# Experts with blocks of 64 slots: raw float32 weights on two column tiles instead of split weights

## The chip, the cores and the metric

The kernel runs on one core of a Trainium2 chip. Its engines are TensorE (PE; its weight loads are a row of their own, PEld), VectorE (DVE), ScalarE (ACT), GpSimd (POOL) and SyncE (SP), which here issues the loads from HBM; 16 DMA engines carry them. The metric is the device time of one execution in microseconds (us).

## The reference, cut to what matters

Two residual layers work on 256 tokens of width 1024 in float32. The change touches only the last part, a layer of eight SwiGLU experts, two for each token:

```python
def moe_swiglu(x, router, w_gate, w_up, w_down):
    t = x.reshape(-1, d)
    top_logits, top_idx = lax.top_k((t @ router), TOP_K)          # 2 of 8
    top_w = jax.nn.softmax(top_logits, axis=-1)
    gates = jnp.sum(jax.nn.one_hot(top_idx, N_EXPERTS) * top_w[..., None], axis=1)
    for e in range(N_EXPERTS):                                    # d = 1024, 3584 inner columns
        out = out + gates[:, e:e+1] * (silu(t @ w_gate[e]) * (t @ w_up[e])) @ w_down[e]
```

The weights of the eight experts are 352 MB of float32, and each is read once.

## The kernel before

**Slots.** The experts are ranked by how many tokens chose them. A rank p has a fixed capacity, `CAPS = (128, 192, 128, 128, 64, 64, 64, 64)`, in blocks of 128 slots ("wide") and of 64 ("narrow"): ranks 0, 2 and 3 have one wide block, rank 1 a wide and a narrow one, ranks 4 to 7 a narrow one each. `gather` (L1155) picks the tokens of a block with matmuls against a 0/1 matrix S (tiles `xgw`, `xgw2` for wide blocks, parts of `fek`, `f1k`, `fak` for narrow ones).

**Order of the work.** A rank's 3584 inner columns are taken in seven column blocks f of 512. `STARTS` says at which step each rank begins; the plan made of it (L234 to L241) is a list of items ("g", p, f), ("u", p, f), ("d", p, f): gate, up and down projection of a column block. Rank 0 comes first, rank 6 joins at its sixth column block and then runs alone, then ranks 1, 4 and 5 run in turn (one column block of each is called a triple below), then 2, 3 and at last 7. Work that follows a projection (evacuations, transposes, scatters) is put some half blocks later by `later(d, ...)` and is issued at `tick()`.

**Weights.** An item reads two weight blocks of 1 MB ("chunks"), each in two halves. SP loads them into eight raw buffers (and at the start into some spare tiles) in the order of the plan; a load waits until the last reader of the buffer's old content is done. `prep` (L138) runs four halves ahead of the use: ACT copies a half, rounded, to `whi` (L146), DVE subtracts to get the rest, `wlo` (L154). PE multiplies both in its faster float32r format, so that the product has nearly full float32 precision.

**Matmuls.** The picked tokens are the stationary operand and the weights stream, 512 columns at a time. A wide block has its tokens split as well and needs three products (`wm`, L412). A narrow block holds 64 high parts and 64 low parts side by side in the 128 columns of the array, so that two products give all four (`streams`, L1198); the two halves of the result lie in different partitions and have to be added. For that each gate and up projection of a narrow block is copied by ACT (`to_rows`, L1220), transposed in four pieces on PE (`folded`, L1237) and summed by DVE's reduction (`summed`, L1242). SiLU and product (`shaped`, L1258 and L1261) and another split (`parted`, L420 and L421) follow; wide blocks are transposed in `turned` (L1267). `down` sums over the column blocks in PSUM or, for a block that "spills", in SBUF (`spilled`), and `scatter` (L1340) brings the sums back to the tokens with S transposed, after they have been split too.

Before the first layer's convolution norm there is `warm_tiles` (L777), a row of matmuls without use on array tiles of 64, 32 and 128 columns.

Of the kernel before, what the change touches and what calls it, by code (L numbers as in the profile page):

```python
# [17 lines left out]
P = 128  # L18
# [35 lines left out]

WARM_TILES = ((64, 256, 5), (32, 256, 3), (64, 512, 3), (128, 256, 2))
# [22 lines left out]
def tile_trunk(ctx: ExitStack, tc: tile.TileContext, a: dict, out: bass.AP, caps=CAPS, starts=STARTS,  # L78
# [94 lines left out]
    def use(count=1):  # L173

        n = state["use"]
        state["use"] = n + count
        if count == 1:
            end = n > 2 * len(chunks) - TAIL
            prep(n + (TAIL_HI if end else LOOK_HI), n + (TAIL_LO if end else LOOK_LO))
            return his[n], los[n]  # L180
        prep(n + count, n + count - 1)
        return [(his[m], los[m]) for m in range(n, n + count)]
# [62 lines left out]
    for p, n0 in starts:  # L245
        kept = [n for n in kept if n + NFB > n0]
        spills[p] = [bi > 0 or len(kept) == 2 for bi in range(len(_blocks(caps[p])))]
        if not spills[p][0]:
            kept.append(n0)
# [15 lines left out]
    for what, p, f in plan:  # L265
        for h in range(2):
            if what == "d":
# [503 lines left out]
    def warm_tiles():  # L771

        b = bank()
        for cols, n, times in WARM_TILES:
            for i in range(times):
                for c in range(0, P, cols):
                    te.matmul(b[c:c + cols, :n], gw[:, i % 4, c:c + cols], m0.rearrange("p g t -> p (g t)")[:, 0:n],  # L777
                              start=True, stop=True)

    def conv_norm(i):  # L780
# [3 lines left out]
        warm_tiles()  # L784
# [315 lines left out]
    def step():  # L1100
        tick()
        return use()
# [43 lines left out]

    def picked(wide):
        i = nth(wide)
        if wide:
            return mop.tile([P, DB, 2 * P], F32R, name="xgw", bufs=1) if i % 2 == 0 else \  # L1150
                fx.tile([P, DB, 2 * P], F32R, name="xgw2", tag="f0")
        pool, tag, h = ((fe, "fe", 0), (fx, "f1", 0), (fx, "f1", 1), (fy, "fa", 1))[i % 4]
        return keep(pool, tag)[:, 2 * h:2 * h + 2, :].rearrange("p a (k s) -> p (a k) s", s=P)

    def gather(p, bi):  # L1155
# [15 lines left out]
        def pick(q):  # L1171
# [6 lines left out]
            later(1, split, xg[:, ks, 0:n], xg[:, ks, n:2 * n], b[:, 0:4 * n].rearrange("p (k f) -> p k f", k=4))  # L1178

        def flip():  # L1180
# [3 lines left out]
            i = nth("sgT") % 5  # L1184
            if p == last or i == 0:
                o = mop.tile([P, T], F32R, name="sgT", bufs=1)
            else:
                o = keep(fe, "fe")[:, 2:4, :].rearrange("p a (k s) -> p (a k) s", s=T)[:, i - 1, :]
            Sg[p, bi] = o
# [8 lines left out]
    def streams(o, l, wide, wh, wl, start, stop):  # L1198
        if wide:
            wm(o, l[:, 0:P], l[:, P:2 * P], wh, wl, start, stop)  # L1200
        else:
            mm(o, l[:, 0:P], wh, start, False)
            mm(o, l[:, 0:P], wl, False, stop)

    sgate, mh = {}, {}

    def project(what, p, f):
        bs = [bank() for _ in blocks[p]]
        for h in range(4):
            wh, wl = step()  # L1210
            for bi, (base, wide) in enumerate(blocks[p]):
                for j in range(2):
                    k = 2 * h + j
                    streams(bs[bi], Xg[p, bi][:, k, :], wide, wh[:, j, :], wl[:, j, :], k == 0, k == DB - 1)
        for bi, (base, wide) in enumerate(blocks[p]):
            later(1, shaped if wide else to_rows, p, f, what, bi, bs[bi])

    def to_rows(p, f, what, bi, b):
        t_ = mop.tile([P, 512], F32, name="row1", bufs=1) if bi else row0()
        se.activation(t_, b, AF.Copy)  # L1220
        later(2, folded, p, f, what, bi, t_)
# [11 lines left out]
    def folded(p, f, what, bi, t_):  # L1233

        b = bank()
        for k in range(4):
            te.transpose(b[:, k * P:(k + 1) * P], t_[:, k * P:(k + 1) * P], ident)  # L1237
        later(1, summed, p, f, what, bi, b)

    def summed(p, f, what, bi, b):  # L1240
        o = late()[:, 1792:2048] if nth("tsum") % 2 else mop.tile([P, 256], F32, name="tsum", bufs=1)
        ve.tensor_reduce(o.rearrange("p (k s) -> p k s", k=4), b.rearrange("p (k h s) -> p k s h", k=4, h=2),  # L1242
                         axis=AX.X, op=OP.add)
        if what == "g":
            later(1, shaped, p, f, what, bi, o)
        else:
            shaped(p, f, what, bi, o)

    def shaped(p, f, what, bi, v):
        n = v.shape[1]  # L1250
        if what == "g":
            if n == 512:
                s = mop.tile([P, n], F32, name="sgate", bufs=1)
            else:
                i = 4 + nth("sgate") % 3
# [6 lines left out]
        later(1, turned if n == 512 else parted, p, f, bi, s)  # L1262

    def turned(p, f, bi, s):
        b = bank()
        for k in range(4):
            te.transpose(b[:, k * P:(k + 1) * P], s[:, k * P:(k + 1) * P], ident)  # L1267
        later(1, parted, p, f, bi, b)

    def parted(p, f, bi, v):  # L1270
        n = v.shape[1] // 4
        y = mop.tile([P, 4, 2 * n], F32R, name="mh", bufs=1) if n == P else part_of(fy, "fb", 4, [4, 2 * n], F32R)
        split(y[:, :, 0:n], y[:, :, n:2 * n], v.rearrange("p (k s) -> p k s", k=4))
# [4 lines left out]
    def down(p, f):  # L1278
        rows = mh.pop((p, f))
        spill = spills[p]  # L1280
        for bi in range(len(blocks[p])):
# [237 lines left out]
```

## Time and profile before

| | |
|---|---|
| time, median of 3 runs | 1474.28 us (1472.83 to 1474.83) |
| profiled execution: its own time | 1477.81 us |
| its span, first to last instruction | 1476.1 us |
| mean granted TensorE clock | 0.979 of 2.4 GHz |
| read from HBM | 418.78 MB, 284 GB/s over the span |
| expert layer, first projection to last | 421 to 1458.7 us |

The profile shows one execution. "Busy" of PE is modelled at its ends, and matmuls are pipelined: a matmul's duration (about 0.4 us) is longer than the distance from its start to the next one's. Costs of matmuls are therefore read from the distance of starts. A raw float32 matmul stands in the trace as two records; a float32r one as one.

### The profile page before, as it was taken

What the parts mean: (1) busy time and instruction counts of PE and PEld (TensorE: products, weight loads), DVE (VectorE), ACT (ScalarE), POOL (GpSimd) and SP (SyncE); (2) the same over time, 40 slices, a digit from 0 to 9 for tenths busy, and PEclk for the clock granted to TensorE, in tenths of its full rate; (3) what the DMA queues carried; (4) which work ended last, traced back from release to release, by engine and by line L of the source; (5) the groups of instructions that cost most, each with busy time, mean ns of one, the idle gap of its engine ahead of it and who ended that gap; (6) DMA issues with size and microseconds to landing.
All of it is one profiled execution on the core that took longest, in us unless ns stands there. A gap on an engine that the chain in (4) does not pass through costs nothing. (4 is left out here: it accounts for less than half of the span.)

```text
span 1476.1 us, 19183 instructions
## 1 busy us (share of the span) xinstructions
PE 1380.9 (94%) x6537; PEld 1098.6 (74%) x6537; DVE 1261.2 (85%) x1553; ACT 977.5 (66%) x1276; POOL 148.3 (10%) x153
## 2 busy tenths in 40 slices
PE   8979999999999999889999999999899999999885
PEld 7648888878887776777778778778767777776553
DVE  6997665787888799888999999999898888878997
ACT  5726555554556688677777877877665667667883
POOL 7923000340110004000000000000000000000001
PEclk9989999999989999899999999999999999999998
DMA  9145662668769798889899999999788989999990
GB/s 341 40 143 200 215 202 69 228 200 280 290 237 339 271 356 287 305 293 341 313 340 357 350 341 351 354 345 353 269 294 297 348 325 325 348 342 327 366 393 35
DMA packets 195380, 421.18 MB, mean 285 GB/s; under 512 B 6832, under 2 KB 42872, under 8 KB 195272
## 3 DMA queue, kind: packets, MB, share of 16 engines
q1 hardware_dynamic: 193496, 414.29, 79.1%
q0 software_dynamic: 1776, 5.56, 1.1%
q8 instruction: 54, 0.88, 0.2%
q14 instruction: 54, 0.44, 0.1%
HBM read 418.78 MB, written 1.05 MB: 284 GB/s over the span
## 5 line engine op out<-in xcount | busy, mean ns | idle before, releaser
L154 DVE TENSOR_TENSOR wlo<-raw,whi 128x1024 fp32r<-128x1024 f32 x773 | 914.0, 1233 | 37.5 <-PE mm L100 17.1
L146 ACT ACTIVATE whi<-raw 128x1024 fp32r<-128x1024 f32 x774 | 762.3, 1050 | 65.0 <-PE mm L100 49.8
L100 PE MATMUL mm<-whi,xgw 128*128 128x512 f32 x896 | 280.8, 394 | 1.0 <-DVE total L1346 1.0
L100 PEld LDWEIGHTS mm<-whi,xgw 128*128 128x128 f32 x896 | 166.9, 188 | 36.7 <-DVE total L1346 1.4
L100 PE MATMUL mm<-wlo,xgw 128*128 128x512 f32 x448 | 177.9, 397 | 10.3 <-DVE wlo L154 10.2
L100 PE MATMUL acc<-whi,mh 128*128 128x512 f32 x448 | 142.8, 400 | 0.0
L100 PE MATMUL mm<-big,whi 128*128 128x512 f32 (+1 forms) x448 | 129.9, 370 | 1.6 <-ACT whi L146 1.6
L100 PEld LDWEIGHTS mm<-wlo,xgw 128*128 128x128 f32 x448 | 84.1, 188 | 37.4 <-DVE wlo L154 17.9
L100 PE MATMUL mm<-wlo,fek 128*128 128x512 f32 x224 | 94.0, 420 | 9.8 <-DVE wlo L154 9.7
L100 PEld LDWEIGHTS acc<-whi,mh 128*128 128x128 f32 x448 | 82.6, 190 | 16.2
L100 PE MATMUL mm<-big,wlo 128*128 128x256 f32 x384 | 92.4, 281 | 0.0
L100 PE MATMUL mm<-whi,fek 128*128 128x512 f32 x224 | 90.9, 406 | 0.0
L100 PE MATMUL mm<-whi,f1k 128*128 128x512 f32 x224 | 90.3, 403 | 0.0
L100 PE MATMUL mm<-wlo,f1k 128*128 128x512 f32 x224 | 88.2, 394 | 0.0
L100 PE MATMUL acc<-wlo,mh 128*128 128x512 f32 x224 | 88.2, 394 | 0.0
L100 PEld LDWEIGHTS mm<-big,whi 128*128 128x128 f32 x448 | 75.6, 194 | 13.3 <-ACT whi L146 2.0
L420 ACT ACTIVATE mh<-mm 128x512 fp32r<-128x512 f32 x28 | 16.7, 596 | 102.5 <-PE acc L100 99.0
L100 PE MATMUL acc<-whi,fbs 128*128 128x512 f32 x168 | 69.4, 413 | 3.1 <-PEq L1375 3.1
L100 PEld LDWEIGHTS mm<-big,wlo 128*128 128x128 f32 x384 | 68.7, 189 | 3.9 <-DVE wlo L154 0.3
L421 DVE TENSOR_TENSOR mh<-mm,mh 128x512 fp32r<-128x512 f32 x28 | 19.3, 691 | 60.8 <-ACT mh L420 60.8
L100 PE MATMUL acc<-wlo,fbs 128*128 128x512 f32 x168 | 68.4, 407 | 2.4 <-DVE wlo L154 2.1
L100 PEld LDWEIGHTS mm<-wlo,fek 128*128 128x128 f32 x224 | 42.5, 190 | 36.1 <-DVE wlo L154 28.5
(305 smaller groups left out, 2037.9 us busy)
## 6 DMA issues: line engine op xcount, KB each, us to landing
raw<-in_odd_moe_w_gate SPq DMA_DIRECT2D x112, 1024.0 KB, 7.2
raw<-in_odd_moe_w_up SPq DMA_DIRECT2D x112, 1024.0 KB, 5.9
raw<-in_odd_moe_w_down SPq DMA_DIRECT2D x110, 1024.0 KB, 7.0
raw<-in_even_ffn_w_gate SPq DMA_DIRECT2D x11, 1024.0 KB, 8.9
raw<-in_even_ffn_w_up SPq DMA_DIRECT2D x11, 1024.0 KB, 5.5
raw<-in_even_ffn_w_down SPq DMA_DIRECT2D x11, 1024.0 KB, 5.0
raw<-in_odd_w_in SPq DMA_DIRECT2D x10, 1024.0 KB, 12.3
raw<-in_even_w_in SPq DMA_DIRECT2D x5, 1024.0 KB, 7.2
```

The costliest lines, as they stand in the source:

```text
L100: te.matmul(o, lhsT, rhs, start=start, stop=stop)
L146: se.activation(his[n], r, AF.Copy)
L154: on.tensor_tensor(los[n], r, his[n].bitcast(F32), op=OP.subtract)
L420: se.activation(dst_hi, y, AF.Copy)
L421: ve.tensor_tensor(dst_lo, y, dst_hi.bitcast(F32), op=OP.subtract)
```

## The change

All projections of a narrow block use the raw float32 weights and unsplit tokens. The 64 tokens are the stationary operand of two tiles of 64 columns of the array, side by side: the left tile streams the left half of a weight row's columns and writes partitions 0 to 63, the right tile the right half and partitions 64 to 127 (256 columns each for gate and up, 512 each for down). So the result of a narrow block is one PSUM bank with 256 (512) columns, with nothing to add. Ranks 4 to 7 need no `whi` and `wlo` any more; rank 1 still does, for its wide block, and its narrow block takes the raw halves. For rank 1 two halves are fetched at once and the wide and the narrow matmuls are grouped (`over_halves`). `to_rows`, `folded`, `summed` and the split of a narrow block's product are gone; the product is transposed in two pieces (`turned`) and copied (`copied`). The scatter of a narrow block is a raw matmul for each half of the columns, with 64 rows (`scatter64`). Narrow sums take one bank instead of two, so that rank 1's narrow block no longer spills. `warm_tiles` is removed. `CAPS`, `STARTS`, the plan and the order of the loads stay.

```diff
-WARM_TILES = ((64, 256, 5), (32, 256, 3), (64, 512, 3), (128, 256, 2))
...
     for what, p, f in plan:
         for h in range(2):
+            if not any(wide for _, wide in _blocks(caps[p])):
+                plain.update((2 * len(chunks), 2 * len(chunks) + 1))
...
     def step():
+
         tick()
-        return use()
+        n = state["use"]
+        return use(), raw_half(n)
...
-            later(1, split, xg[:, ks, 0:n], xg[:, ks, n:2 * n], b[:, 0:4 * n].rearrange("p (k f) -> p k f", k=4))
+            b = b[:, 0:4 * n].rearrange("p (k f) -> p k f", k=4)
+            if wide:
+                later(1, split, xg[:, ks, 0:n], xg[:, ks, n:2 * n], b)
+            else:
+                later(1, se.activation, xg[:, ks, :], b, AF.Copy)
...
+            got = [(h,) + step() for h in (2 * pair, 2 * pair + 1)]
+            for now in (True, False) if pair == 0 else (False, True):
+                for h, w, raw in got:
+                    for bi, wide in enumerate(kinds):
+                        if wide == now:
+                            wide_mm(h, bi, *w) if wide else narrow_mm(h, bi, raw)
...
+        def narrow_mm(h, bi, raw):
+
+            for j in range(2):
+                k = 2 * h + j
+                for c in range(2):
+                    mm(bs[bi][64 * c:64 * c + 64, 0:256], Xg[p, bi][:, k, :], raw[:, j, 256 * c:256 * c + 256],
+                       k == 0, k == DB - 1)
...
-        later(1, turned if n == 512 else parted, p, f, bi, s)
+        later(1, turned, p, f, bi, s)
...
+    def copied(p, f, bi, v):
+
+        y = part_of(fy, "fb", 8, [256], F32)
+        ve.tensor_copy(y, v)
+        mh.setdefault((p, f), {})[bi] = y
...
+            at = j % 2 * P + j // 2 * 64
+            for c in range(2):
+                mm(macc[p, bi][0][64 * c:64 * c + 64, :], rows[bi][:, at:at + 64], raw[:, 0, 512 * c:512 * c + 512],
+                   *ends_of(bi, j))
...
+    def scatter64(p, bi, t):
+        for h in range(2):
+            b, r = bank(), slice(64 * h, 64 * h + 64)
+            mm(b, Sg[p, bi][r, t * P:(t + 1) * P], parts[p, bi][r, :], True, True)
+            later(1, taken, p, t, h, b)
```

How PE's order changes in the triple of ranks 1, 4 and 5: in the kernel before, this is the end of a projection of rank 1 and the one of rank 4 behind it (`xgw_5312` holds the wide tokens of rank 1, `f1k` its narrow ones and rank 4's), with the transposes of a fold (`row_6400`) among the matmuls.

```order
2057 L100 MATMUL mm<-whi,xgw_5312 128x512 x2
2058 L100 MATMUL mm<-wlo,xgw_5312 128x512
2059 L100 MATMUL mm<-whi,f1k 128x512
2060 L100 MATMUL mm<-wlo,f1k 128x512
...
2071 L1237 MATMUL mm<-ident,row_6400 128x128 x4
2072 L100 MATMUL mm<-whi,f1k 128x512
2073 L100 MATMUL mm<-wlo,f1k 128x512
```

The changed kernel at such a place (L98 is the matmul helper, L1284 the transposes of `turned`): the end of a wide group of rank 1, the gate projections of ranks 4 and 5 and a down projection of rank 6 in one stretch on small tiles, then the next wide group; and, a little later, transposes of a narrow product within such a stretch.

```order
1592 L98 MATMUL mm<-wlo,xgw_5065 128x512
1593 L98 MATMUL mm<-raw,f1k 64x256 x32
1594 L98 MATMUL acc<-raw,fbs 64x512 x8
1595 L98 MATMUL mm<-whi,xgw_5065 128x512 x2
...
1618 L98 MATMUL mm<-raw,f1k 64x256 x12
1619 L1284 MATMUL mm<-ident,fdk 128x128 x2
1620 L98 MATMUL mm<-raw,f1k 64x256 x12
```

PE changes between the full array and the small tiles 16 times in a triple, at the wide groups of rank 1 and at each transpose that falls into a narrow stretch; the four transposes of each fold are gone.

On DVE, the last rank (7) in the kernel before, one column block from reduction to reduction:

```order
832 L154 TENSOR_TENSOR wlo<-raw,whi 128x1024 x7
833 L1242 TENSOR_REDUCE tsum<-mm 128x256
834 L154 TENSOR_TENSOR wlo<-raw,whi 128x1024 x4
835 L1242 TENSOR_REDUCE fdk<-mm 128x256
836 L1261 TENSOR_TENSOR fdk<-fdk 128x256
837 L154 TENSOR_TENSOR wlo<-raw,whi 128x1024
838 L421 TENSOR_TENSOR fbs<-fdk,fbs 128x4x64
```

and all that DVE has to do for such a column block in the changed kernel (product, copy):

```order
623 L1277 TENSOR_TENSOR fdk<-mm,fdk 128x256
624 L1295 COPY fbs<-mm 128x256
```

Twelve subtractions, two reductions and the low part of a split leave DVE's queue there, and with the subtractions the raw buffers no longer wait for DVE: PE's matmul is their last reader.

## Rows read from the trace of the kernel before

**Rows 1.** The page: busy time of each engine, its share of the span, instructions

```profile
PE 1380.9 (94%) x6537; PEld 1098.6 (74%) x6537; DVE 1261.2 (85%) x1553; ACT 977.5 (66%) x1276; POOL 148.3 (10%) x153
```

**Rows 2.** Waits of SP's queue, 450 to 1440 us: total us, times, longest

```profile
SPq L128 <- DVE wlo L154: 794.8, 308, 8.9
```

**Rows 3.** Groups by line, whole span: count, busy us, mean ns, idle before

```profile
L154 DVE TENSOR_TENSOR wlo<-raw,whi 128x1024 fp32r<-128x1024 f32 x773 | 914.0, 1233 | 37.5 <-PE mm L100 17.1 <-ACT whi L146 17.0 <-DVEq L1375 2.8
L146 ACT ACTIVATE whi<-raw 128x1024 fp32r<-128x1024 f32 x774 | 762.3, 1050 | 65.0 <-PE mm L100 49.8 <-PE acc L100 4.6 <-DMA raw<-in_even_w_in 4.0
L1242 DVE TENSOR_REDUCE tsum<-mm 128x256 f32<-128x512 f32 x35 | 24.0, 685 | 1.0 <-PE mm L1237 1.0
L1242 DVE TENSOR_REDUCE fdk<-mm 128x256 f32<-128x512 f32 x35 | 23.9, 684 | 0.0
```

**Rows 4.** Stretches: us, busy PE, PEld, DVE, ACT, POOL, granted clock, DMA share, GB/s

```profile
564.80:664.60 99.80, 89.81 (x433) 70.88 (x432) 89.72 (x104) 71.22 (x93) 8.57 (x3) 0.93 0.85 297
664.60:716.70 52.10, 50.56 (x230) 39.76 (x229) 46.79 (x52) 38.57 (x50) 0.00 (x0) 1.00 0.90 315
716.70:1043.70 327.00, 322.49 (x1485) 259.10 (x1483) 306.60 (x329) 248.78 (x303) 0.00 (x0) 1.00 0.98 348
757.00:811.20 54.20, 53.73 (x246) 43.02 (x245) 50.80 (x54) 41.31 (x50) 0.00 (x0) 1.00 0.99 350
1043.70:1329.80 286.10, 269.62 (x1200) 212.78 (x1197) 239.54 (x247) 190.01 (x219) 1.16 (x2) 0.99 0.89 319
1329.80:1458.70 128.90, 112.91 (x458) 76.28 (x456) 120.07 (x125) 97.40 (x120) 0.00 (x0) 0.99 0.83 310
1329.80:1440.00 110.20, 97.84 (x406) 66.27 (x405) 106.16 (x111) 87.76 (x108) 0.00 (x0) 1.00 0.97 361
1384.00:1436.00 52.00, 45.89 (x188) 30.41 (x188) 51.86 (x55) 43.76 (x55) 0.00 (x0) 1.00 1.04 395
```

**Rows 5.** PE in order of time: start, us; first and last of ten

```profile
799.76 0.40 PE L100 MATMUL mm<-whi,fbs 128*128 128x512 f32 x1
...
801.87 0.45 PE L100 MATMUL mm<-wlo,fbs 128*128 128x512 f32 x1
```

**Rows 6.** PE in order of time: raw float32 matmuls of the first layer

```profile
65.78 5.31 PE L100 MATMUL acc<-raw,yb 128*128 128x512 f32 x12
```

**Rows 7.** PE in order of time, from 71.0 us: the warm-up on small tiles

```profile
70.50 0.59 PE L100 MATMUL acc<-raw,yb 128*128 128x512 f32 x1
71.02 2.38 PE L777 MATMUL mm<-m,gw 128*64 128x256 f32 x20
```

**Rows 8.** PE in order of time, from 75 us: the same with 512 columns

```profile
74.76 2.79 PE L777 MATMUL mm<-m,gw 128*64 128x512 f32 x12
```

**Rows 9.** PE in order of time: the four transposes of a fold

```profile
1431.03 0.66 PE L1237 MATMUL mm<-ident,fdk 128*128 128x128 f32 x4 [0.58 <-ACT fdk L1220]
```

**Rows 10.** PE in order of time: sixteen records of a pick

```profile
600.41 1.95 PE L100 MATMUL mm<-S,tok 128*128 128x128 f32 x16
```

**Rows 11.** DVE in order of time: seven subtractions in a row, rank 7

```profile
1390.16 8.03 DVE L154 TENSOR_TENSOR wlo<-raw,whi 128x1024 fp32r<-128x1024 f32 x7
```

**Rows 12.** DVE in order of time: the last subtractions

```profile
1449.89 6.89 DVE L154 TENSOR_TENSOR wlo<-raw,whi 128x1024 fp32r<-128x1024 f32 x6
```

**Rows 13.** After the warm-up: PE's next work, and the stretch from there

```profile
88.15 2.34 PE L792 MATMUL mm<-ident,z 128*128 128x128 f32 x8 [9.53 <-DVE z L787]
...
88.10:94.00 5.90, 5.85 (x13) 3.21 (x14) 5.19 (x12) 2.75 (x3) 5.08 (x3) 0.53 0.00 0
```

**Rows 14.** Weight loads of 64 columns in order of time, then groups of the warm-up

```profile
71.29 0.79 PEld L777 LDWEIGHTS mm<-m,gw 128*64 128x64 f32 x8
...
L777 PEld LDWEIGHTS mm<-m,gw 128*64 128x64 f32 x32 | 2.1, 136 | 2.9 <-issue 2.3
L777 PE MATMUL mm<-m,gw 128*64 128x256 f32 x20 | 2.4, 384 | 0.0
```

**Rows 15.** A stretch within the warm-up, its own instructions (no DVE, ACT, POOL)

```profile
71.25:71.45 0.20, 0.20 (x4) 0.14 (x2) 1.00 1.09 389
```

More of the change, by code (lines that the diff above doesn't have):

```diff
@@ L245, in tile_trunk @@
     for p, n0 in starts:
[L246 to L249, printed above, removed]
+        kept = [(n, k) for n, k in kept if n + NFB > n0]
+        spills[p] = []
+        for _, wide in _blocks(caps[p]):
+            k = 2 if wide else 1
+            spills[p].append(sum(v for _, v in kept) + k > 4)
+            if not spills[p][-1]:
+                kept.append((n0, k))
     if len(passes[-1]) == 1 and caps[last] < P:
@@ L769, in tile_trunk @@
     zn = bt
[L771 to L778, printed above, removed]
     def conv_norm(i):
@@ L783, in conv_norm @@
             return
-        warm_tiles()
         pump(len(bg_v), len(bg_p))
@@ L1145, in keep, with slot64, own, taker @@
         return many[tag]
+    def slot64(i):
+        if i % 4 == 0:
+            return own()[:, 0:512].rearrange("p (k s) -> p k s", s=64)
+        if "f1" not in many:
+            many["f1"] = fx.tile([P, 3, DB, 64], F32, name="f1k", tag="f1")
+        return many["f1"][:, i % 4 - 1]
+    def own():
+        if "fe" not in many:
+            many["fe"] = fe.tile([P, 2048], F32, name="fek", tag="fe")
+        return many["fe"]
     def picked(wide):
         i = nth(wide)
[L1149 to L1153, printed above, removed]
+        if not wide:
+            return slot64(i)
+        return mop.tile([P, DB, 2 * P], F32R, name="xgw", bufs=1) if i % 2 == 0 else \
+            fx.tile([P, DB, 2 * P], F32R, name="xgw2", tag="f0")
+    def taker(p, wide):
+        i = nth(("sgT", wide))
+        if p in (0, last):
+            return mop.tile([P, T], F32R if wide else F32, name="sgT", bufs=1)
+        if not wide:
+            return own()[:, 512 + T * (i % 6):][:, 0:T]
+        return keep(fy, "fa")[:, 2:4, :].rearrange("p a (k s) -> p (a k) s", s=T)[:, i % 4, :]
     def gather(p, bi):
@@ L1183, in flip @@
                 te.transpose(b[:, t * P:(t + 1) * P], G[:, t, :], ident)
[L1184 to L1189, printed above, removed]
+            o = Sg[p, bi] = taker(p, wide)
             later(1, se.activation, o.bitcast(F32) if p == last else o, b[:, :T], AF.Copy)
@@ L1196, in gather @@
         return flip
[L1198 to L1203, printed above, removed]
-    sgate, mh = {}, {}
[L1207 to L1221, printed above, removed]
+    sgate, mh = {}, {}
     def late():
```

115 lines of the change are left out of this document (71 added, 44 removed).

## Prediction, made before the changed kernel was run

> **What bounds the kernel now.** I read the busy line, the waits of the transfer queue, the groups by line, the table of stretches, and then the time-ordered rows for the prices. Of 1476.1 us TensorE (PE) is busy 94%, VectorE (DVE) 85% [rows 1]. The expert layer fills the stretch from 421 us on. There the queue that loads weights waits 794.8 us for DVE's subtraction at L154, the last reader of a raw block [rows 2]: the transfers follow DVE. The two splits run over every weight half (773 on DVE, 774 on ScalarE, ACT); the folding of the 64-slot blocks adds 70 reductions [rows 3] and as many copies. The table of stretches [rows 4] cuts the layer into five, at times at which the last projection of a pass has been read out (the copy at L1220 or the product at L1261):
> - W1, 564.8 to 664.6, rank 6 (64 slots) almost alone: DVE busy 89.7 of 99.8 us, transfers at 297 GB/s, granted clock 0.93 (part of it at 1.2 GHz). DVE holds it.
> - W2, 664.6 to 1043.7, ranks 1, 4 and 5 in turn: in its steady part, 54.2 us for a triple of column blocks, PE is busy 53.7 and DVE 50.8. Both are at their limit, PE first.
> - W3, 1043.7 to 1329.8, ranks 2 and 3 (128 slots), which keep their splits.
> - W4, 1329.8 to 1458.7, rank 7 (64 slots): DVE 120.1 of 128.9 us. From 1384 to 1436 the transfers run at 395 GB/s with a DMA share of 1.04, the fastest this trace shows for so long.
> - W5, the last 17.4 us, the final norm.
>
> **Prices.** A split-weight matmul of 512 columns: ten of them start between 799.76 and 801.87, 9 steps in 2.11 us [rows 5], 0.234 us; I take 0.233. A raw float32 matmul is two records: twelve records of 512 columns last 5.31 us with an end of 0.59 [rows 6], so (5.31-0.59)/11 = 0.429 each, 0.858 a matmul. For two column tiles the old kernel has a sample, its warm-up: 20 records of 64x256 on two tiles take 2.38 us, of which 0.38 is the last one's own [rows 7, 14], so ten pairs start 0.22 apart; twelve of 64x512 take 2.79 [rows 8], (2.79-0.59)/5 = 0.44 a pair with the slower first one. One tile after the other would be double. I take 0.216 per pair of 256-column records (half of 0.429), so 0.432 us for a pair of matmuls and 0.858 for a pair of 512 columns. A change of tile shape: the first small tile starts 0.52 after the matmul before it, which needs 0.429, so 0.09 [rows 7]. Four transposes take 0.66 us [rows 9], 0.16 each with the last one's end in it; I take 0.11, the step of the pick records, which have its size: 16 of them in 1.95 us [rows 10], 0.112 without the end.
>
> **The change part by part.** Split halves go from 773 to 437 on DVE, at 1.13 us each ((8.03-1.23)/6 [rows 3, 11]): 380 us of DVE work and about 350 of ACT's vanish, with the 70 folds on both. That is worth only what PE and the transfers then allow, stretch by stretch.
>
> W1. PE's need before: 248 split matmuls x 0.233 = 57.8, 128 pick records x 0.112 = 14.3, 8 of the scatter = 1.9, 46 transposes x 0.11 = 5.1, together 79.1 of 99.8 us; the other 20.7 is waiting for DVE and the clock it loses. After: 24 x 0.233 = 5.6, 80 pairs x 0.432 = 34.6, 16 pairs x 0.858 = 13.7, picks and scatter 16.2, 16 transposes 1.8, 38 changes of tile shape x 0.09 = 3.4: 75.3. With 2.7 left for waits 78, so **-22**. The transfers must bring 30 blocks of 1.049 MB, at 395 GB/s 2.66 us each, 80 us; eight blocks lie ready in the raw buffers, so they do not bind here.
>
> W2. Before: 1472 x 0.233 = 343.0, 198 transposes 21.8, picks 3.6, scatter 1.9: 370.3 of 379.1. After: 480 x 0.233 = 111.8, 336 pairs x 0.432 = 145.2, 80 pairs x 0.858 = 68.6, 74 transposes 8.1, picks 3.6, 4 raw scatters 3.4, 116 changes of shape 10.4: 351.1. With 6 of the 8.8 us of waits kept, 357: **-22**. A triple comes to 50.3 us on PE (72 x 0.233, 48 x 0.432, 12 x 0.858, 10 transposes, 16 changes) against 18 blocks x 2.66 = 47.9 of transfers: PE stays the bound, DVE falls to about a third.
>
> W3. The splits of the wide ranks stay, and so does their rhythm. The 64-slot sums are now scattered by 12 raw matmuls (10.3 us) where split ones took 5 to 7; some of DVE's late work at the start of this stretch goes. I take **+3**, between -6 and +6.
>
> W4. PE's need falls to 92 us (48 x 0.233, 112 x 0.432, 28 x 0.858, the rest 8) and DVE has next to nothing. What is late next is the transfer: from 1329.8 to 1440.0 it moved 110.2 us x 361 GB/s = 39.8 MB [rows 4]. At 395 GB/s that is 100.7 us, then the last half block is multiplied: 104 against 128.9, **-25**. In the old kernel the last bytes are there by 1440 and DVE still has six subtractions to do, until 1456.8 [rows 12]; that queue is gone.
>
> The rest. Behind the warm-up matmuls at 71 us PE waits 9.5 us for DVE, until 88.15, and the clock is at 0.53 from 88.1 to 94 in spite of them [rows 13]. Without them that wait is longer and the low clock may last until 97, at most +2; PE work is taken from in front of a wait for DVE, which gains nothing: I take 0. The start of the layer before 564.8 holds two column blocks of rank 6 beside rank 0, PE-bound: -1. The new waits of PE on raw blocks have nothing behind them but later blocks. New small work (a copy of 128x256 on DVE and one on ACT per column block) lies on engines that are now two thirds idle. W5 unchanged.
>
> Sum: -1 -22 -22 +3 -25 = -67. The profiled execution took 1477.8 us, 3.5 above the median of the runs; the sum goes on the median: 1474.3 - 67 = **1407 us**.
>
> [...] The rows show weight loads of 64 columns, eight of them in the 0.79 us from 71.29 on, in which the small tiles keep their step [rows 7, 14]: the loads are hidden. [...]
>
> **Rivals.**
> 1. The narrow pairs run slower than the sample, at the 0.233 us of a split matmul, because the two tiles now stream different columns of a block while it is being written around them; and a change of shape costs twice. W1 and W2 hold 1216 steps of 0.216: +20, and 154 changes: +15. 1427 to 1442. For it: every split matmul in this layer is above 0.215. Against: the sample kept its step while transfers ran at 389 GB/s [rows 15].
> 2. **Slower:** the two tiles run one after the other. In the sample both tiles read the same moving tensor; here each has its own 256 or 512 columns, which no row shows. Then a step is 0.43: W2 gains 992 steps x 0.216 = 214 us, W1 48, W4 becomes PE-bound at 92 + 73 = 165, the rest about 27: 1407 + 214 + 48 + 61 + 27 = 1757. It decides from a step of about 0.263 on: 1216 steps, 128 elsewhere and 336 in W4 beyond its 12 us of slack then eat the 67 us.
> 3. The loads are exposed: 0.136 us a load [rows 14] on 832 record pairs in W2, 192 in W1, 280 in W4 less its 12 us of slack, 96 elsewhere: 113 + 26 + 26 + 13 = 178, 1585.
> 4. The transfers do not hold 395 GB/s: at the 350 of W2, W4 takes 117 and W2 about 360: 1423.
> 5. DVE's relief also smooths W3 and the waits in W2: 1392.
>
> **How the numbers follow.** Forecast 0.58 (1395 to 1421), rival 1 0.17, rival 4 0.07, rival 5 0.07, rival 2 0.06, rival 3 0.03, and 0.02 that gains and new waits cancel. 0.2% is what a measurement here can tell from no change. Slower: 0.09; same: 0.02; faster: 0.89. The range 1388 to 1442 leaves out rivals 2 and 3 and the tails.
>
> **What would show it.** Pairs of records on the two tiles starting within some ns, then 0.216 later; 437 subtractions; the steady triple at 50 to 51 us with PE still over 95% busy and DVE under half; W1 near 78 us with the clock at 1.00; W4 near 104 us with DMA at 1.0 throughout and PE waiting for raw blocks. A pair step over 0.26, a W2 over 379 us, or a W4 in which PE waits for anything but a transfer would make the prediction wrong.

## The result, and the profile after

The changed kernel takes **1420.1 us** (median of 4 runs, 1418.4 to 1421.3) against 1473.6 of the kernel before on the same chip (1471.5 to 1474.8): a ratio of 0.9638, 95% interval 0.9621 to 0.9655, so 53 us less. 67 less were forecast, 1407 us; 1420 lies in the range of 1388 to 1442. The profiled execution of the changed kernel took 1419.3 us, its span is 1417.5, 58.6 less than the span before. (The profiled execution before was 4.3 us above this median of before, the one after 0.9 below its own; that is the difference between 58.6 and 53.)

The busy line of the page, which answers to [rows 1]:

```profile
PE 1330.3 (94%) x7387; PEld 944.7 (67%) x7387; DVE 817.1 (58%) x1108; ACT 602.7 (43%) x830; POOL 136.9 (10%) x153
```

VectorE's (DVE's) share falls from 85 to 58%, ScalarE's (ACT's) from 66 to 43; TensorE (PE) keeps its 94% in a span that is 4% shorter. Then the waits of the transfer queue in the expert layer, as [rows 2] (total us, times, longest):

```profile
SPq L126 <- PE mm L98: 299.3, 130, 9.4
SPq L126 <- DVE wlo L152: 277.9, 108, 8.4
SPq L126 <- PE acc L98: 104.3, 46, 7.5
```

The wait for the subtraction was 794.8 us and is 277.9; now the queue waits longer for PE (299.3 and 104.3 us), the last reader of a raw block that a narrow block uses. The groups by line, as [rows 3], with the narrow matmuls and their weight loads:

```profile
L152 DVE TENSOR_TENSOR wlo<-raw,whi 128x1024 fp32r<-128x1024 f32 x437 | 522.8, 1244 | 170.7 <-ACT whi L144 153.1
L144 ACT ACTIVATE whi<-raw 128x1024 fp32r<-128x1024 f32 x438 | 432.6, 1050 | 76.2 <-DMA raw<-in_odd_moe_w_up 37.5
...
L98 PE MATMUL mm<-raw,f1k 128*64 128x256 f32 x1344 | 154.8, 383 | 0.0
...
L98 PEld LDWEIGHTS mm<-raw,f1k 128*64 128x64 f32 x1344 | 92.7, 137 | 55.9 <-issue 12.8
```

The subtractions are 437, as counted, the copies 438. The table of stretches, as [rows 4]; W1 to W5 end at the same places of the program as before (the product of the pass's last up projection starts, for W4 the last weight matmul has ended):

```profile
560.60:638.80 78.20, 77.95 (x562) 47.93 (x558) 15.88 (x31) 12.49 (x23) 0.00 (x0) 1.00 0.98 358
638.80:1000.80 362.00, 358.26 (x2260) 213.76 (x2259) 128.94 (x153) 97.79 (x123) 0.00 (x0) 1.00 0.99 361
736.00:788.15 52.15, 51.48 (x322) 30.60 (x322) 18.09 (x22) 13.78 (x17) 0.00 (x0) 1.00 0.99 361
1000.80:1283.00 282.20, 269.91 (x1195) 203.25 (x1194) 222.94 (x227) 177.29 (x203) 1.15 (x2) 1.00 0.91 329
1283.00:1399.70 116.70, 100.18 (x640) 51.23 (x638) 16.98 (x27) 8.65 (x15) 0.00 (x0) 0.97 0.91 341
1283.00:1297.00 14.00, 14.00 (x98) 9.99 (x97) 5.36 (x6) 5.15 (x7) 0.00 (x0) 1.00 0.73 252
1297.00:1389.00 92.00, 75.48 (x512) 38.51 (x510) 11.62 (x22) 3.50 (x8) 0.00 (x0) 0.98 1.03 393
1389.00:1399.70 10.70, 10.70 (x34) 2.73 (x32) 0.00 (x0) 0.00 (x0) 0.00 (x0) 0.82 0.03 12
1399.70:1417.50 17.80, 2.74 (x10) 1.09 (x8) 12.91 (x26) 3.19 (x5) 4.92 (x4) 0.69 0.16 59
```

Against the forecast, stretch by stretch of the profiled executions:

| stretch | before | forecast | after |
|---|---|---|---|
| W0, up to rank 6 alone | 564.8 | 563.8 | 560.6 |
| W1, rank 6 | 99.8 | 78 | 78.2 |
| W2, ranks 1, 4, 5 | 379.1 | 357 | 362.0 |
| its triple of column blocks | 54.2 | 50.3 | 52.15 |
| W3, ranks 2, 3 | 286.1 | 289 | 282.2 |
| W4, rank 7 | 128.9 | 104 | 116.7 |
| W5, final norm | 17.4 | 17.4 | 17.8 |

W1 came out to the microsecond, W2 and W4 fell short by 5 and 13, W3 and W0 were better by 7 and 3.

The narrow pairs, in order of time on PE and on its weight loads, 32 records, the four halves of one item of rank 1:

```profile
646.01 3.67 PE L98 MATMUL mm<-raw,f1k 128*64 128x256 f32 x32
```
```profile
646.01 3.22 PEld L98 LDWEIGHTS mm<-raw,f1k 128*64 128x64 f32 x32 [0.36 <-issue]
```

16 pairs in 3.67 us with 0.38 us for the last one's own end and 0.05 for a slower first one: 3.24 / 15 = 0.216 us a pair, the price taken from the warm-up. In the single records the second tile's matmul starts 6 or 7 ns after the first tile's. The last of the 32 weight loads ends 0.45 us before the last matmul, and the pairs keep their step: the loads are hidden, as in the sample.

The end of W4 is the place that the forecast missed most. PE in order of time, with its idle time and what ended it:

```profile
1379.79 3.10 PE L98 MATMUL acc<-raw,fbs 128*64 128x512 f32 x12
1387.84 1.97 PE L98 MATMUL acc<-raw,fbs 128*64 128x512 f32 x4 [4.95 <-PEq L1428]
1389.75 2.08 PE L98 MATMUL acc<-total,ident 128*128 128x512 f32 x2
...
1394.36 5.37 PE L98 MATMUL acc<-raw,fbs 128*64 128x512 f32 x24
```

PE stands 4.95 us at L1428, the branch that tests whether a rank holds more tokens than slots (the branch itself lasts 6.1 us in PE's queue). Behind it four records take 1.97 us where, at 1394.36, twenty-four take 5.37: from 1386.1 to 1392.9 the granted clock is 0.5 of full speed (the trace gives this share and no frequency; it is what the recorded texts call 1.2 GHz). The transfers are done at 1389 (12 GB/s from there on in the table), but PE has 7 pairs of matmuls and two matmuls of the residual still to do and needs 10.7 us for them.

### The profile page after: what moved, and what is told of

Same layout as the page of the kernel before. It is cut to its first block, busy times and chain, and to the rows that moved or that the text cites. A ratio compares the mean times of both kernels' runs of the same rounds, so it can differ in the third digit from the quotient of the medians.

```text
span 1417.5 us, 19418 instructions
## 1 busy us (share of the span) xinstructions
PE 1330.3 (94%) x7387; PEld 944.7 (67%) x7387; DVE 817.1 (58%) x1108; ACT 602.7 (43%) x830; POOL 136.9 (10%) x153
## 5 line engine op out<-in xcount | busy, mean ns | idle before, releaser
L152 DVE TENSOR_TENSOR wlo<-raw,whi 128x1024 fp32r<-128x1024 f32 x437 | 522.8, 1244 | 170.7 <-ACT whi L144 153.1
L144 ACT ACTIVATE whi<-raw 128x1024 fp32r<-128x1024 f32 x438 | 432.6, 1050 | 76.2 <-DMA raw<-in_odd_moe_w_up 37.5
L98 PE MATMUL mm<-whi,xgw 128*128 128x512 f32 x896 | 283.4, 397 | 0.0
L98 PEld LDWEIGHTS mm<-whi,xgw 128*128 128x128 f32 x896 | 165.0, 188 | 49.1 <-issue 12.6
L98 PE MATMUL mm<-wlo,xgw 128*128 128x512 f32 x448 | 177.6, 396 | 11.4 <-DVE wlo L152 11.4
L98 PE MATMUL mm<-raw,f1k 128*64 128x256 f32 x1344 | 154.8, 383 | 0.0
L98 PE MATMUL acc<-whi,mh 128*128 128x512 f32 x448 | 142.8, 400 | 0.0
L98 PE MATMUL mm<-big,whi 128*128 128x512 f32 (+1 forms) x448 | 131.0, 374 | 1.6 <-ACT whi L144 1.6
L98 PEld LDWEIGHTS mm<-raw,f1k 128*64 128x64 f32 x1344 | 92.7, 137 | 55.9 <-issue 12.8
L98 PE MATMUL mm<-raw,fek 128*64 128x256 f32 x896 | 105.5, 383 | 9.0 <-DMA raw<-in_odd_moe_w_up 5.1
L98 PE MATMUL acc<-raw,fbs 128*64 128x512 f32 x448 | 106.5, 608 | 7.3 <-PEq L1428 5.0
L98 PEld LDWEIGHTS mm<-wlo,xgw 128*128 128x128 f32 x448 | 84.2, 188 | 36.7 <-DVE wlo L152 18.3
L98 PEld LDWEIGHTS acc<-whi,mh 128*128 128x128 f32 x448 | 81.0, 188 | 26.0 <-issue 5.6
L98 PEld LDWEIGHTS mm<-raw,fek 128*64 128x64 f32 x896 | 62.3, 137 | 49.1 <-issue 7.4
L98 PE MATMUL mm<-big,wlo 128*128 128x256 f32 x384 | 92.6, 282 | 0.0
L98 PE MATMUL acc<-wlo,mh 128*128 128x512 f32 x224 | 87.7, 391 | 0.0
L98 PEld LDWEIGHTS mm<-big,whi 128*128 128x128 f32 x448 | 76.6, 197 | 13.4 <-ACT whi L144 2.0
L1277 DVE TENSOR_TENSOR fdk<-mm,fdk 128x256 f32<-128x256 f32 x35 | 14.7, 421 | 104.1 <-PE mm L98 104.1
L98 PEld LDWEIGHTS mm<-big,wlo 128*128 128x128 f32 x384 | 69.0, 190 | 3.9 <-DVE wlo L152 0.4
L98 PEld LDWEIGHTS acc<-raw,fbs 128*64 128x64 f32 x448 | 29.0, 138 | 63.3 <-issue 56.8
L1274 ACT ACTIVATE sgate<-mm 128x512 f32<-128x512 f32 x28 | 16.8, 598 | 113.5 <-PE mm L98 113.5
```

The source lines that it names most:

```text
L98: te.matmul(o, lhsT, rhs, start=start, stop=stop)
L144: se.activation(his[n], r, AF.Copy)
L152: on.tensor_tensor(los[n], r, his[n].bitcast(F32), op=OP.subtract)
L1274: se.activation(s, v, AF.Silu)
L1277: ve.tensor_tensor(s, v, s, op=OP.mult)
```

## The experiments

Each run changes the changed kernel. Ratios are to the kernel before on the same chip; the changed kernel has 0.9638 (0.9621 to 0.9655).

**Does VectorE's relief pay, or TensorE's shorter work?** The splits of the narrow ranks put back, into tiles that nobody reads:

```diff
-            if not any(wide for _, wide in _blocks(caps[p])):
-                plain.update((2 * len(chunks), 2 * len(chunks) + 1))
```

> The changed kernel, but ScalarE and VectorE still split the weights of the 64-slot ranks, into tiles that nobody reads (336 halves each): the raw matmuls stay, the relief of the two engines is taken back. Theory: with TensorE's shorter narrow work and the folding gone VectorE has room for them (a narrow column block is 12 x 1.13 = 13.6 us of VectorE beside 15.6 of TensorE or 16 of transfers, a triple 44 of 52): W2 unchanged, W1 and W4 a few us more, 1420 to 1432 us. Rival: the relief of VectorE is what the change gains in W1 and W4, and W1 goes back to 99 and W4 to 129: 1450 to 1456.

Measured: 1470.0 us, 0.9965 (0.9938 to 0.9992). The theory fell. The raw matmuls are all there, and still some 48 of the 53 us are lost, by the ratios. The rival, 1450 to 1456, was too low and had only part of the place: W1 takes 90.3 and not 99, and the most is lost in W2, where it expected nothing (W1, W2 and a steady triple of this run):

```profile
559.40:649.70 90.30, 82.47 (x553) 50.16 (x554) 78.98 (x87) 63.19 (x78) 3.00 (x2) 0.94 0.88 314
649.70:1037.50 387.80, 364.98 (x2260) 215.35 (x2261) 313.88 (x319) 254.83 (x289) 0.00 (x0) 0.99 0.94 336
811.60:867.70 56.10, 52.07 (x325) 30.81 (x325) 45.69 (x48) 36.64 (x41) 0.00 (x0) 1.00 0.96 344
```

DVE is busy 81% of W2, so it is not full. What PE waits for over the whole run (total us, times, longest):

```profile
PE mm L1282 <- DVE fdk L1275: 40.0, 23, 4.7
```

That is the product of gate and up projection (the narrow form), which PE needs for the next transposes; in the changed kernel this line is 4.2 us. The splits also read weights that must have arrived, wait for each other (in W2 a subtraction for its copy, 42.3 us in all), and hold raw blocks (over the run the queue waits 598.1 us for the subtraction, 513.7 in the changed kernel). To take that away and leave the work, the same pieces were made to read tokens that lie in SBUF:

```diff
+            elif n in idle:
+                se.activation(hip.tile([P, D], F32R, name="whi"), X[:, 0, :], AF.Copy)
...
+            elif n in idle:
+                ve.tensor_tensor(lop.tile([P, D], F32R, name="wlo"), X[:, 0, :], X[:, 1, :], op=OP.subtract)
```

> As the run that kept the splits of the 64-slot ranks (1470 us), but each of these copies and subtractions reads tokens that lie in SBUF all along in place of the weights: as much work at the same places of the two queues, with no wait for a transfer and none of the subtraction for the copy; raw blocks are released by TensorE alone. Its results are not used. Theory A: what costs is the wait that the splits bring into the two in-order queues and the hold on raw blocks; without it the work fits: 1421 to 1435 us. Theory B: the busy time of VectorE itself costs, small work (product, copy) queues behind 1.2 us pieces whatever they read: 1460 to 1470 us.

Measured: 1467.6 us, 0.9945 (0.9927 to 0.9962). Theory B: the wait for the product is 40.1 us in 23 waits, the same as with the splits themselves, though no piece waits for a transfer. Then each engine by itself; first ACT's copies of the narrow weights kept, without the subtractions:

> The changed kernel with ScalarE's copies of the 64-slot weights kept (336, unread) and VectorE's subtractions gone: which of the two engines' relief pays. If VectorE's: 1420 to 1428 us. If ScalarE's queue (a SiLU that waits for TensorE holds the copies behind it, and copies that wait for a transfer hold the SiLU): 1445 to 1470 us.

Measured: 1424.8 us, 0.9664 (0.9638 to 0.9690): ACT's 336 copies cost some 4 us by the medians, and the intervals, which overlap, leave open whether anything. Then DVE's idle subtractions without ACT's idle copies:

> As the run with resident work (1467.6 us), but with VectorE's 336 idle subtractions alone; ScalarE's idle copies are gone. Theory: VectorE's time is what the relief is worth, and products queued behind pieces of 1.2 us are how it reaches TensorE: 1455 to 1468 us, and TensorE's waits for the narrow product (line of the product in shaped) stay at 30 to 40 us. Rival: it takes both engines (a SiLU behind copies, a subtraction behind a SiLU): 1425 to 1440 us.

Measured: 1465.0 us, 0.9907 (0.9880 to 0.9934); PE's wait for the narrow product:

```profile
PE mm L1287 <- DVE fdk L1280: 40.1, 23, 4.7
```

So it is nearly all DVE's work. DVE in order of time shows how, in this run between two narrow products, that of rank 1 (it starts at 802.49) and that of rank 4, with one item of 64 slots of PE's between them:

```profile
802.82 2.35 DVE L154 TENSOR_TENSOR wlo<-tok 128x1024 fp32r<-128x1024 f32 x2
805.09 0.68 DVE L427 TENSOR_TENSOR mh<-mm,mh 128x512 fp32r<-128x512 f32 x1
805.69 0.41 DVE L1298 COPY fbs<-mm 128x256 f32<-128x256 f32 x1
806.02 2.35 DVE L154 TENSOR_TENSOR wlo<-tok 128x1024 fp32r<-128x1024 f32 x2
808.28 0.42 DVE L1280 TENSOR_TENSOR fdk<-mm,fdk 128x256 f32<-128x256 f32 x1
```

in the changed kernel, from the product of rank 1 to that of rank 4 in the triple that ends at 788.15:

```profile
780.11 0.41 DVE L1277 TENSOR_TENSOR fdk<-mm,fdk 128x256 f32<-128x256 f32 x1
781.74 0.69 DVE L424 TENSOR_TENSOR mh<-mm,mh 128x512 fp32r<-128x512 f32 x1 [1.21 <-ACT mh L423]
782.34 0.41 DVE L1295 COPY fbs<-mm 128x256 f32<-128x256 f32 x1
784.08 0.42 DVE L1277 TENSOR_TENSOR fdk<-mm,fdk 128x256 f32<-128x256 f32 x1 [1.32 <-PE mm L98]
```

With the idle subtractions DVE never rests: four pieces of 1.14 us, the split of the wide rows (0.6), the copy and the product, 5.79 us from product to product. Without them it rests 1.21 and 1.32 us, and the products are 3.97 apart, which is PE's own time. What PE makes of the first, in order of time: it stands 1.50 us before the transposes of the late product, then 2.03 before the next one's:

```profile
808.76 0.44 PE L1287 MATMUL mm<-ident,fdk 128*128 128x128 f32 x2 [1.50 <-DVE fdk L1280]
```

Rests of 2.5 us an item would take two pieces and not four. So the question was whether it is the pace inside a run of narrow items that counts, or each piece:

```diff
-                idle.update((2 * len(chunks), 2 * len(chunks) + 1))
+                idle.add(2 * len(chunks))
```

> As the run with VectorE's idle subtractions alone (1465.0 us, 45 over the changed kernel), but for every second half block only: 168 in place of 336. Theory: what counts is the pace within a run of narrow halves, where a subtraction of 1.14 us a half is slower than TensorE's 0.87 (4 matmuls of two records on two tiles), so that the products at the end of the run are late; at one in two halves, 0.57 us a half, VectorE keeps up and hardly anything is lost: 1420 to 1428 us, waits for the narrow product under 12 us. Rival: each subtraction costs its share, whatever the pace: 1420 + 22 = 1440 to 1446 us.

Measured: **1420.5 us**, 0.9616 (0.9580 to 0.9652), the changed kernel's time. 168 subtractions of 1.2 us cost nothing that these runs can tell (the interval is 5 us wide to either side); 336 cost 40 us by the ratios, 45 by the times. The same place in this run, and PE's waits for the narrow product over the whole run:

```profile
783.85 1.22 DVE L154 TENSOR_TENSOR wlo<-tok 128x1024 fp32r<-128x1024 f32 x1
785.14 0.69 DVE L427 TENSOR_TENSOR mh<-mm,mh 128x512 fp32r<-128x512 f32 x1
785.75 0.41 DVE L1298 COPY fbs<-mm 128x256 f32<-128x256 f32 x1
786.08 1.21 DVE L154 TENSOR_TENSOR wlo<-tok 128x1024 fp32r<-128x1024 f32 x1
787.48 0.42 DVE L1280 TENSOR_TENSOR fdk<-mm,fdk 128x256 f32<-128x256 f32 x1 [0.18 <-PE mm L98]
```
```profile
PE mm L1287 <- DVE fdk L1280: 4.3, 8, 0.7
```

Two pieces fill the rests, DVE still waits 0.18 us for PE, and the triple is 52.1 us again (from rank 4's product to that of the next triple, 787.5 to 839.6). Relief has a threshold here, not a price per piece: 1420.5 us with 168 pieces put back, 1465.0 with 336.

**What do the pairs depend on?** The two loops of the narrow projections swapped, so that neighbours in the program are on the same tile:

```diff
-            for j in range(2):
-                k = 2 * h + j
-                for c in range(2):
+            for c in range(2):
+                for j in range(2):
+                    k = 2 * h + j
```

> The changed kernel with the two loops around the narrow projections swapped, so that two matmuls on the same column tile follow each other (tile 0, 0, 1, 1 in place of 0, 1, 0, 1); the down projections keep their order. Theory: TensorE takes matmuls in order and only neighbours on different tiles run side by side; four matmuls take 3 steps in place of 2. 80 pairs in W1, 336 in W2, 32 in W0, half a pair step of 0.432 more each: 17 + 73 + 7 = 97; in W4 transfers hide it: 1420 + 97 = 1517 us (1490 to 1530). Rival: each tile has its own queue, order does not matter: 1420, within 4 us. Second rival: with the order changed nothing overlaps, 4 steps: 1420 + 194 = 1614 or more.

Measured: 1420.3 us, 0.9627 (0.9593 to 0.9662). The first rival was right: order does not matter. In the trace each tile's records still start 0.216 us apart; only the two tiles' starts lie 13 or 58 ns apart in place of 6. So in this run each column tile kept the pace of 0.216 us with two matmuls in a row on one tile; longer runs were not tried.

**What does a change of tile shape cost?** Rank 1's halves not grouped by kind:

```diff
-            if len(set(kinds)) == 1:
+            if True:
```

> The changed kernel without the grouping of halves by kind for rank 1 (128 + 64 slots): each half block goes through the split matmuls and then through the narrow pairs, so an item changes tile shape 7 times inside in place of 2 or so. 21 items x 5 to 6 more changes = 105 to 126. Theory: a change costs 0.09 us going wide and 0.14 going narrow (0.115 mean): +12 to +14.5, the triple 54.0 to 54.3 in place of 52.15: 1432 to 1435 us. Rival: the changes fall into waits and cost nothing: 1420, within 3 us.

Measured: 1429.4 us, 0.9686 (0.9653 to 0.9719), 9 us more; W2 takes 372.4 in place of 362.0 and its triple 53.55. The count was too high: the records show 80 changes between split and narrow matmuls to narrow and 74 to wide where the changed kernel has 39 and 34, 81 more, 0.13 us of W2 each. The price was too low, for PE does not rest in this W2:

```profile
637.20:1009.60 372.40, 372.40 (x2260) 206.76 (x2259) 130.18 (x154) 98.55 (x124) 0.00 (x0) 1.00 0.97 351
```

The changed kernel is busy 358.26 there and idle 3.74, so the 81 changes cost PE 14.1 us of work, 0.17 each, 3.7 of it in time in which it would have waited. The steps show what most of it is made of: 0.09 at the switch in either direction, 0.05 more for the first pair of a narrow stretch (0.267 in place of 0.216), and 0.10 more for the first split matmul behind one (0.335 in place of 0.231). The grouping that the change brings with it is worth these 9 us.

**The end.** The branch two items earlier (`IF_AT = 3`), where PE waits for transfers anyway:

> The changed kernel with the test for overfull experts (a branch on every engine) two items earlier, before the last up projection of rank 7 in place of before the second last down projection. Theory: in the changed kernel TensorE stands 4.95 us at this branch (1382.9 to 1387.8), loses its clock to 1.2 GHz there and then has 8 pairs of 512-column matmuls left when the last weights land at about 1389; earlier, the same wait falls where TensorE waits for transfers anyway. The last weight matmul moves from 1399.6 to about 1391: 1420 - 8 = 1412 us (1410 to 1415). Rival: the end is set by the transfers and what follows them, and the branch only covers that: 1420, within 2 us. Second rival: the drain of pending work in front of the branch exposes a product and its transposes: 1422 to 1426.

Measured: 1416.7 us, 0.9596 (0.9562 to 0.9629): less than half of what was expected, and the interval overlaps that of the changed kernel. The stand of PE moved but did not shrink (the profile names ACT's queue; PE's own branch lasts 6.3 us there), the 32 records behind it take 5.89 us in place of 3.67, and PE was late from there to the end:

```profile
1368.42 3.18 PE L98 MATMUL mm<-raw,fek 128*64 128x256 f32 x24
1377.44 5.89 PE L98 MATMUL mm<-raw,fek 128*64 128x256 f32 x32 [5.85 <-ACTq L1428]
```

The price of the branch as a whole, by leaving it and the code behind it out:

> The changed kernel without the test for overfull experts and its branch (the path that would compute tokens beyond a rank's slots is left out; with these inputs it isn't taken). The last weights are still requested ahead, at the same place. Theory: TensorE's 4.95 us at the branch and its slow clock behind it are the 8 to 10 us by which the stretch of rank 7 outlasts its transfers, so the last weight matmul ends at about 1391 in place of 1399.6 and the kernel takes 1411 us (1408 to 1414), lower than the 1416.7 with the branch two items earlier, where TensorE still stood 5.85 us and had its backlog until 1396. Rival: the backlog is the work behind the late weights themselves, the branch only fills it: 1416 to 1420.

Measured: 1409.7 us, 0.9550 (0.9525 to 0.9575), 10 us less, within what was expected. PE's last weights are done at 1391.5, some 3 us behind the transfers, and the granted clock is 1.00 from 1384 to 1392:

```profile
1386.11 5.37 PE L98 MATMUL acc<-raw,fbs 128*64 128x512 f32 x24
```

Then the branch kept, early, but over a shorter body: the loop over the 8 experts in the skipped code as a loop on the chip.

```diff
-IF_AT = 1
+IF_AT = 3
...
-            for e in range(NE):
+            with tc.For_i(0, NE, 1) as e:
```

> The changed kernel with the test for overfull experts two items earlier (1416.7 us alone) and with the code that the branch skips made about eight times shorter: its loop over the 8 experts is a loop on the chip in place of 8 copies. Theory: the 6 us that TensorE stands at the branch are the fetch of code behind a long jump; with a short one it stands 1 to 2 us and the kernel takes 1411 us (1409 to 1414), near the 1409.7 without any branch. Rival: the wait is that of any jump taken while the transfers are saturated: 1415 to 1418.

Measured: **1414.6 us**, 0.9565 (0.9541 to 0.9589), faster than the changed kernel (the intervals do not touch) and 4.3% faster than the kernel before. The time lies just above the theory's range and below the rival's, and its interval overlaps that of the early branch alone; what the short body does is read from the trace. PE's branch lasts 0.36 us in place of 6.0 to 6.3, with the transfers at 390 GB/s during it, which speaks against the rival, and PE stands 1.10:

```profile
1372.56 1.95 PE L98 MATMUL mm<-raw,fek 128*64 128x256 f32 x16 [0.15 <-DMA raw<-in_odd_moe_w_gate]
1375.60 1.95 PE L98 MATMUL mm<-raw,fek 128*64 128x256 f32 x16 [1.10 <-ACTq L1428]
1377.89 1.95 PE L98 MATMUL mm<-raw,fek 128*64 128x256 f32 x16 [0.35 <-DMA raw<-in_odd_moe_w_up]
```

The other engines' queues show the same: from the branch to the next step 5.2 us on ACT and 5.5 on DVE in the changed kernel, 0.4 and 0.5 here. The traffic of the instruction queue tells what PE seems to wait for. During PE's branch in the changed kernel that queue brings one piece of 16 KB, which starts 3.6 us into the branch, takes 1.1 and ends 1.5 before the branch does. Every trace with the long body has such a piece, which ends 1.4 to 1.7 us ahead of the branch's end; with the short body no piece falls into the branch. In the kernel before, where the transfers are over (10 GB/s during the branch), the piece starts 1.0 us into it, and the branch lasts 3.4.

What remains above the 1409.7 (the intervals overlap) is put down to the small waits of the queues at L1428 and the work that drains in front of it; no run parts them. With these inputs no rank has more tokens than slots, so the skipped code did not run in any of these kernels.

Last, rank 7 started five passes earlier, beside rank 3, with the branch two items earlier:

```diff
-STARTS = ((0, 0), (6, 5), (1, 12), (4, 12), (5, 12), (2, 19), (3, 26), (7, 33))
+STARTS = ((0, 0), (6, 5), (1, 12), (4, 12), (5, 12), (2, 19), (3, 26), (7, 28))
```

> The changed kernel with rank 7 started in pass 28 in place of 33, so that five of its column blocks run beside those of rank 3, and the branch two items earlier. Theory: rank 7 alone is bound by transfers (16 us a column block, TensorE 10.9), rank 3 alone by TensorE (20.2 us, transfers at 329 GB/s); a pair takes 32 us at 395 GB/s in place of 36.2: 5 x 4.2 = 21 us less, 3 for the branch, some lost to changes of tile shape: 1420 - 20 = 1400 us (1393 to 1408). Rival: beside rank 3 the raw blocks are released by VectorE's splits and the transfers stay at 330 to 360 GB/s: 1412 to 1420.

Measured: 1418.3 us, 0.9602 (0.9578 to 0.9627): nothing beyond the earlier branch. The first four of the five pairs, what follows them up to the end of the weights, and both together:

```profile
1194.40:1311.00 116.60, 114.73 (x612) 78.78 (x610) 65.34 (x65) 51.88 (x60) 0.00 (x0) 1.00 0.98 368
1311.00:1405.00 94.00, 79.09 (x421) 44.90 (x420) 31.59 (x39) 20.43 (x25) 0.00 (x0) 0.91 0.80 303
1194.40:1405.00 210.60, 193.82 (x1032) 123.68 (x1030) 96.93 (x104) 72.31 (x85) 0.00 (x0) 0.96 0.90 339
```

against the changed kernel from rank 3's second column block to the end of the transfers:

```profile
1188.40:1389.00 200.60, 179.69 (x1015) 120.17 (x1014) 93.85 (x104) 70.80 (x85) 0.00 (x0) 0.99 0.96 357
```

These pairs run well, 29.2 us each with PE 98% busy and the transfers at 368 GB/s. But PE has 180 us of work in the 201 us of the changed kernel, so there was idle time of 21 us to win and not what the sum of stages promised. In this run the last two blocks of rank 7 are left alone at the end, take 14 and 26 us (a 6.4 us stand at the branch in the second) and lose the clock (0.91 granted).

**The warm-up.** WARM_TILES and its matmuls put back:

> The changed kernel with the removed warm-up matmuls (WARM_TILES, 7.5 us of TensorE at 71 us) put back. In the changed kernel TensorE now waits 17.0 us for VectorE's z in place of 9.5, and the clock is at 1.2 GHz from 75.4 to 95.8 in place of 83.4 to 93.6. Theory: VectorE sets the pace there (39 of 40 us busy), the warm-up bought nothing: 1420, within 2 us. Rival: the low clock delays the matmuls behind z: 1416 to 1418 us.

Measured: 1416.7 us, 0.9598 (0.9570 to 0.9626), an interval that overlaps that of the changed kernel. PE's wait for DVE's z, in the changed kernel and in this run:

```profile
PE mm L785 <- DVE z L780: 17.0, 1, 17.0
```
```profile
PE mm L797 <- DVE z L792: 9.5, 1, 9.5
```

From the first raw matmul of the layer before to the first one behind this wait it is 27.6 us in the kernel before, in the changed kernel and here, and to the next stage's first matmul 69.6, 69.6 and 69.7. So the warm-up buys nothing at its place, though by the time alone the rival's 1416 to 1418 came true. The profiled run is 2.7 us ahead of the changed kernel's at the last down projection of rank 6 before W1 (544.19 and 546.90), hundreds of us behind the warm-up; five other runs, without the warm-up and with the same code up to there, lie between 545.30 and 550.80. So differences of that size come without a cause in the code, and whether the 3 us of the median are real stays open.

## Why the prediction was right, and where it was off

- **W1: right.** DVE held it, PE's need was put at 75.3 with 2.7 for waits, and it took 78.2 with the clock at 1.00. PE was busy 77.95 of it: the 2.7 us went into dearer work and not into waits, so that the exact figure is in part luck.
- **The pair: right**, on every term: 0.216 a pair, loads hidden, tiles side by side with different columns. Rivals 1 to 3 fall with that. The second one (tiles one after the other, 1757) rested on a sample in which both tiles read the same columns; different columns changed nothing. The third rested on weight loads that come on top; 137 ns loads lie beside pairs of 216 ns here, on two tiles that both use all 128 rows, and the last of 32 loads ends 0.45 us before the last matmul. What was shown is this for tiles of 64 columns; how a load gets in beside the matmuls was not.
- **W2: PE's need of 351.1 us was too small.** The waits are 3.7 us, less than the 6 that were taken: in six of the seven triples PE starts 0.6 us late, for rank 5's product, ahead of which DVE has three wide subtractions. But PE is busy 358.3 us. A change of shape costs the 0.09 of the forecast at the switch and then 0.05 more in the first pair (57 stretches, 2.9 us) or 0.10 more in the first split matmul behind it (33 places, 3.4 us), so that the term of 10.4 us for the changes is nearer 17. So 362.0 and not 357.
- **W2, why it could fall at all.** The prediction gave the gain to PE ("PE first") and let DVE's relief be worth what PE allows. The runs show what it did not price: with the narrow splits kept beside PE's shorter work W2 becomes longer, 387.8. DVE's need there, by pace and not by share, is above what PE then wants (5.79 against 3.97 us from one narrow product to the next). 21.5 of PE's 22.8 us of idle time in that W2 are waits for the narrow product; why the old order, in which PE idled 6 us and W2 took 379.1, suffered less was not settled. The other half, DVE's relief with the old work on PE, was not run: PE was busy 373 of those 379.1 us [rows 4], so W2 could hardly have fallen by relief alone; that is worked out and not measured.
- **W3: the term "12 raw matmuls (10.3 us)" was a little too large, and the late work of DVE was given no figure.** In the scatter the two halves of 64 rows can run two at a time: 16 of the 24 records start in pairs, 5 to 7 ns apart, with 0.53 to the next pair; the other 8 ran alone. Together they take 8.7 us, 0.4 of it a wait. The larger part of the way from +3 to -3.9 is idle time: PE is busy 269.6 us before and 269.9 after, and its idle time falls from 16.5 to 12.3.
- **W4: two steps failed.** "At 395 GB/s that is 100.7 us": from 1297 on the transfers kept 393, but for the first 14 us they made 252, because the raw blocks of rank 3's last projections came free from DVE's subtractions and PE one by one (the queue waits 8.3 us for the one and 7.7 for the other from 1278 to 1297); 106 us in all, +5. "Then the last half block is multiplied": a tail of 3 us was taken, it is 10.7. The branch was in the profile before, beside a DVE that was later still, and was given no line:

```profile
1447.70 0.48 PE L100 MATMUL acc<-whi,fbs 128*128 128x512 f32 x1 [3.07 <-PEq L1375]
```

- **W4, the branch.** With DVE gone it became the latest thing in W4, and dearer. Leaving it out gave back 10 us. The prediction had named a W4 in which PE waits for anything but a transfer as a sign that it is wrong; for this stage the sign came.
- **Rival 4** named nearly the times of W2 and W4 (360 and 117 us; 362.0 and 116.7 came) and 1423 us in all, nearer than 1407, but by slower transfers. In W4 these ran at 393 GB/s from 1297 to 1389, and in W2, at 361, PE was busy 358.3 of 362.0 us. That its figures fit is luck.
- **The sum.** -4.2, -21.6, -17.1, -3.9, -12.2, +0.4: 58.6 of the span. Set on the median of before, from a profile that was itself some 4 us above it, it counts for 53. So of the 13 us that are missing some 8 lie in the stages and 5 in setting the sum on the median. That 1420 still lies in the narrower range of 1395 to 1421 is in part luck: W2 and W4 missed by 18 us together, and W0 and W3 gave 10 of them back for other reasons.
- The signs to look for held for the pairs, the 437 subtractions, W1, DVE under half in the triple (18 of 52) and PE waiting for raw blocks in W4; the triple was 52.15 and not 50 to 51, W4 116.7 and not 104, with the DMA share at 0.73 in its first 14 us and not at 1.0 throughout.

## What to carry to other kernels

An engine that is 80% busy over a stretch can still set its pace, as DVE did with the narrow splits kept (81% busy in a W2 of 387.8 us, where 362.0 do without them): compare its time with the other engine's within a run of like items, where small work that the other engine needs queues behind the large pieces. Relief had a threshold here: with half of the subtractions put back the kernel took 1420.5 us, as the changed kernel does (1420.1), with all of them 1465.0; so measure how much is needed before more is built. And when the engine that was last is taken away, walk through the end of the stage for one-off stalls that it had covered, such as the branch here (PE stands 4.95 us).

## What the hardware showed that was not expected

- The branch over the long body took 6.0 to 6.3 us on PE with the 8 experts written out and transfers running, 3.4 with the transfers over (the kernel before), 0.36 with the body a loop. That the time is the fetch of the code behind the jump is the author's reading. A piece of 16 KB in the instruction queue falls into each long branch and none into the short one, which fits it; which engine a piece is for the profile does not tell, so the cause was not shown.
- With two matmuls in a row on one column tile of PE, the order in the program made no difference (1420.3 and 1420.1 us; 0.216 us from record to record on each tile in both).
- Two matmuls on different halves of the rows started side by side too (16 of the 24 records of the scatter in W3, 5 to 7 ns apart; why the other 8 ran alone was not settled).
- A change between 128 and 64 columns cost more than the 0.09 us at the switch: with the slower first step behind it (0.05 for a narrow pair, 0.10 for a split matmul) 81 more changes cost PE 0.17 us each.
- 168 subtractions of 1.2 us on DVE could be added to the changed kernel without a difference that these runs can tell (1420.5 us).
